# A macaron transformer block: order of the casts and seeds in the paired feed-forward phases, values first in the mixer, and the last head's casts placed a chunk later

## Chip, cores and metric

The kernel runs on one core of a Trainium2 chip. The metric is device time in microseconds (us) for one execution. Three runs of the kernel before took 935.04, 937.92 and 938.45 us, median 937.92 us.

## What is computed

One block for 512 tokens of width 1024, all float32: half a SwiGLU feed-forward network of width 2816, a token mixer with eight heads, again half a feed-forward network, and an RMS norm.

```python
def swiglu(x, w_gate, w_up, w_down):
    return (jax.nn.silu(x @ w_gate) * (x @ w_up)) @ w_down

x = x + 0.5 * swiglu(rmsnorm(x, ffn1_norm[layer]), ...)
x = x + token_mixer(rmsnorm(x, mix_norm[layer]), w_in[layer], w_out[layer], ...)
x = x + 0.5 * swiglu(rmsnorm(x, ffn2_norm[layer]), ...)
return rmsnorm(x, final_norm)
```

In the mixer `x @ w_in` gives queries, keys and values. Four differential heads form `a = p0 - lam * p1` from two softmaxes with a relative bias and apply it to the values (`oa`, followed by an RMS norm per head). Eight small heads sum three dilated attention branches (`ob`). The concatenated heads are multiplied with `w_out`.

## The kernel before

**Arithmetic.** Activations lie transposed, as eight tiles `x[0]` to `x[7]` of 128 features by 512 tokens. To keep float32 accuracy each operand is split in a high part (a cast to the reduced type, on ScalarE, `A`) and a low part (the operand minus that cast, on VectorE, `V`). A product is then three matmuls on TensorE (`T`): high by high, high by low, low by high (`mm3`, L124 to L126). So every weight needs a cast and a subtraction before its phase: `high` (L383) and `low` (L387) in the feed-forward networks, `high` (L854) and `low` (L858) in the mixer.

**Feed-forward networks (`ffn`).** After some ordinary units the network works on pairs of row blocks with seven half-width products in place of eight, a Winograd scheme. One unit has seven phases of 12 matmuls of 256 columns each:

```python
SEVEN = (("a11", "w", "b11"), ("s3", "z", "t3"), ("s2", "x", "t2"), ("a12", "w", "b21"),
         ("s1", "y", "t1"), ("a22", "x", "t4"), ("s4", "y", "b22"))
```

The first name is the weight block or sum, the second the PSUM bank (`pw`, `px`, `py`, `pz`) that it accumulates in, the third the activation block. After a11 bank w is copied as a seed into bank x, and after s2 bank x into bank y (`A.copy`, reported at L412). So s2 waits for the first seed and s1 for the second; s4, which accumulates in y, also waits until VectorE has read y after s1 (L415 in a gate or up unit, L424 in an output unit). Units come as `("g", j)` gate, `("u", j)` up, `("p", m)` plain output and `("d", group, m)` paired output. All of it is put in order by a list of planned times: `at(time, rank, f)` pushes a step on a heap, `put` is rank 0, `starts[t]` is the planned start of phase t, and `STEP` (1410 ns) the planned length of a phase. Steps come out by time, then by rank, then by the order in which they were pushed, and each engine runs its own steps in that order. Nothing waits for the planned time itself. At one time the ranks before are: 0 the reading of banks, seeds, activations and casts of gated results; 1 loads and the low parts `t0_rest` and `t1_rest`; 2 weight sums (`total`, L365 and L367) and the gate's `silu` of bank w; 2.5 `low`; 3 `high`; 4 `product`, the matmuls. `high` stands four steps ahead of its phase and `low` three.

In a gate unit `silu(0, left)` reads bank w a step after a12, and `silu(1)` the sum in `res["bc"]` a step after a22; the up unit multiplies them in later (`mul`, `stt`). `kept` makes the operands of the output units from the gated result. There `t0_parts` (reported at L557) casts a difference that VectorE has just formed (L421).

**Mixer.** The work is a list of chunks of 6 matmuls of 512 columns (queries and keys, `qk_chunks`, 8 chunks for each of `q0` to `q7`) or 12 of 256 columns (values, `v_chunks`, 8 for each of `v0` to `v3`), in the order of `plan`. Chunk c of `v_chunks` computes token block `c // 2` with weight half `c % 2`, so one bank is in work at a time. Around the chunks events are placed by chunk number: `put(t, rank, f)`, ranks below 10 ahead of the chunk, others behind it. After each chunk one half of a weight unit is cast (`high`) and the low part of the one before is formed.

After the chunks of `q{u}`, `scaled` brings queries and keys out of PSUM with the norm's factors (tq at L933, tk at L935, VectorE). Then heads 0 and 7 (`DIRECT`) run `evac_now`: four casts for each of two halves (L965, L967, L968 and L970) on ScalarE, and two subtractions for each (L966, L969) on VectorE, all queued right behind the last chunk. The other heads run `evac_q` (four casts) and `evac_k` (two subtractions of keys, L956, two of queries, L959, and copies between partitions by DMA). `attention(u, s)` then places scores (`sc`, L1002 and L1003), the biased row maximum with its subtraction (L1005, VectorE), the exponential (L1008, ScalarE), `combine` (L1012 to L1019), `turn` (transposes `pt`, L1026, and their copy `ptb`, L1029, ScalarE), `values` (`po`, L1039), `scale`, `finish` (`ot`, L1075, and the cast of `mh`) and `finish_low`. Head u starts at chunk s; its strips of the bias are loaded by two DMAs of SyncE's queue at chunk s - 3. Scores use two PSUM buffers, and so do transposes.

`means` and `spread` (`rstd`) work out the norm's factors. `means` makes the column `col` that scales the values and the diagonal `dg`; `spread` multiplies `dg` with ones (`bc_n`, L193) and copies the result to `bc`, which scales queries and keys. They stand at chunks 3 and 6.

After the last queries come `w_out` chunks (`pwo`) between which the last two heads run. The casts of some later `w_out` units (L115, L116) are placed by the scheduler of the framework, not by the list.

Of the kernel before, what the change touches and what calls it, by code (L numbers as in the profile page):

```python
# [65 lines left out]
def tile_macaron(ctx: ExitStack, tc, xs, xT, wf, wgu1, wst1, wd1, wdg1, wqk, wv, wo, wgu2, wst2, wd2,  # L66
# [132 lines left out]
    def ffn(wgu, wst, wd, wdg, n0, n1, norm, early, res, nm, hooks, ended, first=None,  # L199
# [206 lines left out]
        def put(time, f, *a):  # L406
            at(time, 0, f, *a)
# [18 lines left out]
        def product(t):  # L426
            u, o = ops[t]
            h, l = made.pop(t)
            if o[0] == "p":
                m = u[1]  # L430
                po = mm_bank(f"pd{nm}{m}")
                for k in range(PLAIN):
                    c = slice(k * P, (k + 1) * P)
                    mm3(po[:], h[:, c], l[:, c], ah[k][:], al[k][:], k == 0, k == PLAIN - 1)
                put(starts[t + 1], stt, x[m], po[:], 0.5, x[m], ALU.add)
                return
            if t == begin[u]:
                made[u] = {}
                for b, tag in zip("wxyz", bank_tags(u)):
                    made[u][b] = pp.tile([P, S], F32, tag=tag, name=f"p{b}{u[0]}{nm}{t}",  # L440
                                         bufs=4 if tag == "mm" else 2)[:, :HS]
            banks = made[u]
            seeded = o[0] not in ("a11", "s3")
            if t == 0 or ops[t - 1][1][0] == "p":
                T.matmul(banks[o[1]][:, :P], h[:, :P], moving(u, o[2])[0][0][:, :P],
                         start=True, stop=False, skip_group_check=True)
            for p, mv in enumerate(moving(u, o[2])):
                c = slice(p * P, (p + 1) * P)
                mm3(banks[o[1]], h[:, c], l[:, c], *mv, not seeded and p == 0, p == 3, seeded)


            if o[0] == "a11":
                put(starts[t + 1], A.copy, banks["x"], banks["w"])
            elif o[0] == "s2":
                put(starts[t + 1], A.copy, banks["y"], banks["x"])
            elif u[0] == "d":
                down_step(starts[t + 1], u, o[0], banks)
            else:
                pair_step(starts[t + 1], u, o[0], banks)
# [8 lines left out]
        def pair_step(t, u, o, banks):  # L468
# [15 lines left out]
            elif u[0] == "g":  # L484


                if o == "a12":
                    if j == n1:
                        put(t, silu, 0, left, pw)
                        put(t + STEP, times_up, 0, left)  # L490
                    else:
                        at(t + STEP, 2, silu, 0, left, pw)
                elif o == "s1":
                    put(t, add, res["bc"][:, right], py, p7)
                elif o == "a22":
                    put(t, add, p7, px, p7)
                    put(t + STEP * (j > n1), silu, 1, slice(0, S), res["bc"][:], -1.0)
                elif o == "s4":
                    put(t, silu, 0, right, py)
                    if j == n1:  # L500
# [16 lines left out]
        def kept(j, t1, t0, t2):  # L517
# [61 lines left out]
            put(n, less, g0[:, left], g0[:, left], g0[:, right])  # L579
            put(n + STEP, b2_rest)  # L580
            put(n + STEP, less, g0[:, right], g1[:, right], g0[:, right])
            put(n + 2 * STEP, t0_parts)
            put(n + 2 * STEP, stt, g1[:, right], g1[:, right], -1.0, g0[:, left], ALU.subtract)
            put(n + 2 * STEP, stt, g1[:, left], g1[:, right], -1.0, g1[:, left], ALU.subtract)

# [27 lines left out]
        def pipeline():  # L613
            seen = {}
            for t, (u, o) in enumerate(ops):
# [4 lines left out]
                else:  # L620
# [13 lines left out]
                    if o[0] in ("s2", "s4"):  # L634
                        at(starts[t] - 5 * STEP, 2, total, t)
                    at(starts[t] - 4 * STEP, 3, high, t)
                    at(starts[t] - 3 * STEP, 2.5, low, t)
                at(starts[t], 4, product, t)
            if bias is not None:
                at(starts[begin["p", 5]], 5, bias[0])  # L640
# [187 lines left out]
    V.tensor_scalar_mul(sub8[:], sm[:, 4 * KD:4 * KD + 1], 1.0 - LAM0)  # L828


    plan = ["q0", "v0", "q1", "v1", "q2", "q3", "q4", "v2", "q5", "q6", "v3", "q7"]
    v_end = [8 * plan.index(f"v{u // 2}") + 8 for u in range(8)]
    at = {}

# [43 lines left out]
    def v_chunks(qr):  # L878
# [2 lines left out]
        st = {}  # L881

        def chunk(c):
            i, kh = c // 2, c % 2
            if c == 0:
                ahead(us[0])
            if kh == 0:
                st["ps"] = mm_bank(f"pv{qr}{i}")
            po = st["ps"][:, :256]
            wh, wl = ready[us[kh]]  # L890
            xs = slice(i * P, (i + 1) * P)
            if c == 0:
# [6 lines left out]
            if kh == 1:  # L899
                if hf == 0:  # L900
                    vt[vi, i] = slot(vi * 4 + i, f"v{vi}{i}")
                A.activation(vt[vi, i][:, hf * 256:hf * 256 + 256], po, AF.Copy,
                             scale=held["col"][:, i:i + 1])
            if c == 7:
                ahead(us[1])
        return [lambda c=c: chunk(c) for c in range(2 * NQ)]

# [3 lines left out]
    def qk_chunks(u):  # L911
# [48 lines left out]

        def evac_now():
            q0, q1, k0, k1, l0, l1 = tiles()
            tq, tk = scaled()
            for a, b, qx, kx, lx in ((lo, hi, q0, k0, l0), (hi, lo, q1, k1, l1)):
                A.copy(qx[a, :], tq[a, :])  # L965
                V.tensor_tensor(qx[b, :], tq[a, :], qx[a, :].bitcast(F32), op=ALU.subtract)  # L966
                A.copy(kx[a, :], tk[a, :])  # L967
                A.copy(kx[b, :], tk[a, :])  # L968
                V.tensor_tensor(lx[a, :], tk[a, :], kx[a, :].bitcast(F32), op=ALU.subtract)  # L969
                A.copy(lx[b, :], lx[a, :].bitcast(F32))  # L970

        e = 8 * plan.index(f"q{u}") + 7
        if u in DIRECT:
            put(e, 11, evac_now)
        else:
            put(e, 11, evac_q)
            put(e + 1, 11, evac_k)
# [4 lines left out]
    def attention(u, s):  # L982
# [39 lines left out]
        def turn(m, i):  # L1022
# [3 lines left out]
                T.transpose(pt[:, k * P:(k + 1) * P],  # L1026
                            st["pr"][m][:, OFF[i] + k * P:OFF[i] + (k + 1) * P], ident[:])
            ptb = tp.tile([P, S], F32, tag="ptb", name=f"ptb{u}{m}{i}", bufs=2)
            A.copy(ptb[:, :w], pt[:, :w])  # L1029
            st["ptb", m, i] = ptb  # L1030

        def values(m, i):
# [63 lines left out]
        for i in range(NQ):  # L1096
# [2 lines left out]
            put(s + step * i + (1 if quick else 3), 5, combine, i)  # L1099
            if diff:  # L1100
                put(tv + 2 * i, 2, turn, 0, i)
                put(tv + 2 * i + 2, 1, values, 0, i)
            else:
                for m in range(2):
                    put(tv + step * i + (0 if quick else m), 2, turn, m, i)
# [11 lines left out]
        else:  # L1117
            put(e, 7, scale)
        put(e + (0 if quick else 2), 11 if quick else 3, finish)
        put(e + (0 if quick else 3), 12 if quick else 8, finish_low)  # L1120

    for w in plan:
        chunks += (qk_chunks if w[0] == "q" else v_chunks)(int(w[1]))
        if w[0] == "q":
            attention(int(w[1]), len(chunks) + (3 if int(w[1]) in DIRECT else 5))

    WO = 3
    wo_units = [unit(wo[m], f"wo{m}") for m in range(KD)]
# [19 lines left out]

    means, spread = rstd("n2", held)
    put(3, 9, means)  # L1150
    put(6, 9, spread)

    load(0)
    load(1)
# [215 lines left out]
```

## Time and profile before

| | |
|---|---|
| median of three runs | 937.92 us |
| the profiled execution, own time | 934.85 us |
| its span, first to last instruction | 933.1 us |
| VectorE busy | 723.9 us (78%) |
| ScalarE busy | 532.0 us (57%) |
| DMA moved | 136.71 MB, mean 147 GB/s |

In the rows of the trace the first number is the start in us from the beginning of the span and the second the duration. PE is TensorE, DVE is VectorE, ACT is ScalarE and SP is SyncE. A bracket at the end names idle time of that engine ahead of the row and what ended it. Matmuls overlap: a row's end is modelled, so the distance between two starts tells more than a duration. The stages by time: first feed-forward network to about 341 us, mixer to about 560, then the rest of `w_out` and the second network, whose paired phases run from 647 to 919 us, and the final norm.

### The profile page before, as it was taken

How to read it: one execution, taken by the hardware profiler on the slowest of the kernel's cores; microseconds unless marked ns; L12 is line 12 of the kernel's file. 1: busy time of each engine (PE TensorE's matmuls, PEld its weight loads, DVE VectorE, ACT ScalarE, POOL GpSimd, SP SyncE). 2: the span in 40 equal slices, each digit the busy share in tenths (PEclk: the TensorE clock that was granted, in tenths of full speed). 3: DMA queues.
4: the chain of work that ended last, by engine and by line, in shares of the span. 5: the costliest groups of instructions: out<-in, count | busy, mean ns of one | idle time of the engine just before them, and what ended most of it. 6: DMA issues, size and time to landing. Idle time of an engine off the chain costs nothing.

```text
span 933.1 us, 17213 instructions
## 1 busy us (share of the span) xinstructions
PE 916.4 (98%) x6462; PEld 848.4 (91%) x6462; DVE 723.9 (78%) x1490; ACT 532.0 (57%) x1102; POOL 98.3 (11%) x117
## 2 busy tenths in 40 slices
PE   9999999999999999999999999999999999999995
PEld 7788999999999998988989888888999899999995
DVE  6697897687997896668764537597899778798786
ACT  7455664355664665566756645355666445666462
POOL 0011101112102100000000002201110102220100
PEclk9999999999999999999999999999999999999997
DMA  7176646578757641443333103345775667874832
GB/s 251 65 194 157 167 127 176 137 195 223 195 150 193 188 128 65 131 136 113 91 113 92 68 23 117 121 136 142 177 171 137 175 168 178 216 215 124 209 103 91
DMA packets 60388, 136.71 MB, mean 147 GB/s; under 512 B 6848, under 2 KB 9152, under 8 KB 60304
## 3 DMA queue, kind: packets, MB, share of 16 engines
q1 hardware_dynamic: 46304, 110.14, 35.8%
q0 software_dynamic: 14000, 25.47, 17.4%
q8 instruction: 50, 0.82, 0.4%
q14 instruction: 34, 0.28, 0.1%
HBM read 130.30 MB, written 2.14 MB: 142 GB/s over the span
## 4 chain that ended last, share of the span: by engine, by line
PE 91%; DVE 6%; ACT 2%; issue 1%; DMA 1%; SPq 0%; DVEq 0%
PE po L1039 3%; PE pwo L124 1%; PE pwo L125 1%; PE pwo L126 1%; PE pua L126 1%; PE pua L125 1%; PE pua L124 1%; PE pv L896 1%; PE pv L897 1%; PE pv L898 1%; PE pt L1026 1%; PE pq L124 1%; PE pq L126 1%; PE pq L125 1%; PE pdb L124 1%; PE pda L124 1%
## 5 line engine op out<-in xcount | busy, mean ns | idle before, releaser
L1005 DVE CUSTOM_DVE_ANT_0 pr<-sc,strip 128x128 f32<-128x128 f32 (+3 forms) x64 | 30.9, 488 | 34.8 <-PE sc L1003 34.2
L1008 ACT ACTIVATE pr<-pr,small 128x128 f32<-128x128 f32 (+3 forms) x64 | 36.0, 563 | 32.1 <-DVE small L1005 31.2
L383 ACT CAST w<-s2b 128x512 fp32r<-128x512 f32 x50 | 31.1, 622 | 14.1 <-DVE s2b L365 12.7
L383 ACT CAST w<-s2a 128x512 fp32r<-128x512 f32 x46 | 28.7, 623 | 15.9 <-DVE s2a L365 13.3
L151 POOL TENSOR_TENSOR sq<-sq,sqt 128x512 f32<-128x512 f32 x7 | 10.9, 1559 | 254.4 <-ACT sqt L150 254.4
L387 DVE TENSOR_TENSOR w<-s2b,w 128x512 fp32r<-128x512 f32 x50 | 34.3, 686 | 4.3 <-ACT w L383 4.3
L1039 PEld LDWEIGHTS po<-v,ptb 128*128 128x128 f32 x240 | 32.7, 191 | 5.3 <-ACT ptb L1029 2.7
L896 PE MATMUL pv<-w,xh 128*128 128x256 f32 x128 | 35.9, 281 | 0.0
L897 PE MATMUL pv<-w,xl 128*128 128x256 f32 x128 | 35.8, 280 | 0.0
L898 PE MATMUL pv<-w,xh 128*128 128x256 f32 x128 | 35.7, 279 | 0.0
L387 DVE TENSOR_TENSOR w<-s2a,w 128x512 fp32r<-128x512 f32 x46 | 31.5, 686 | 3.9 <-ACT w L383 3.9
L1039 PE MATMUL po<-v,ptb 128*128 128x64 f32 (+1 forms) x240 | 32.5, 269 | 1.8 <-ACT ptb L1029 1.7
L1029 ACT COPY ptb<-pt 128x128 f32<-128x128 f32 (+3 forms) x48 | 20.0, 424 | 20.2 <-PE pt L1026 19.9
L124 PE MATMUL pq<-xh,w 128*128 128x512 f32 x64 | 26.9, 421 | 0.0
L124 PE MATMUL pwo<-mh,w 128*128 128x512 f32 x64 | 26.1, 407 | 0.0
L125 PE MATMUL pwo<-ml,w 128*128 128x512 f32 x64 | 25.5, 399 | 0.0
L126 PE MATMUL pwo<-mh,w 128*128 128x512 f32 x64 | 25.5, 398 | 0.0
L124 PE MATMUL pk<-xh,w 128*128 128x512 f32 x64 | 25.1, 393 | 0.0
L125 PE MATMUL pq<-xl,w 128*128 128x512 f32 x64 | 25.1, 392 | 0.0
L126 PE MATMUL pq<-xh,w 128*128 128x512 f32 x64 | 25.1, 392 | 0.0
L126 PE MATMUL pk<-xh,w 128*128 128x512 f32 x64 | 25.0, 391 | 0.0
L125 PE MATMUL pk<-xl,w 128*128 128x512 f32 x64 | 25.0, 390 | 0.0
(671 smaller groups left out, 3973.8 us busy)
## 6 DMA issues: line engine op xcount, KB each, us to landing
raw_qk<-wqk_dram SPq DMA_DIRECT2D x16, 512.0 KB, 3.5
raw0bg<-wst_dram SPq DMA_DIRECT2D x9, 512.0 KB, 4.6
raw_gua<-wgu_dram SPq DMA_DIRECT2D x8, 512.0 KB, 3.9
raw0ag<-wst_dram SPq DMA_DIRECT2D x8, 512.0 KB, 4.8
raw0ad<-wdg_dram SPq DMA_DIRECT2D x8, 512.0 KB, 5.0
strip<-bias_rows SPq DMA_DIRECT2D x16, 256.0 KB, 3.5
raw_v<-wv_dram SPq DMA_DIRECT2D x8, 512.0 KB, 3.2
raw_wo<-wo_dram SPq DMA_DIRECT2D x8, 512.0 KB, 3.2
```

The lines of the kernel that those rows point to most:

```text
L124: T.matmul(po, wh, mh, start=first, stop=False, skip_group_check=on)
L125: T.matmul(po, wh, ml, start=False, stop=False, skip_group_check=on)
L126: T.matmul(po, wl, mh, start=False, stop=last, skip_group_check=on)
L383: A.copy(made[t][0], source(t))
L387: V.tensor_tensor(l, source(t), h.bitcast(F32), op=ALU.subtract)
L896: T.matmul(po, xh[k][:, xs], wh[:, o:o + 256], start=k == 0, stop=False)
L897: T.matmul(po, xl[k][:, xs], wh[:, o:o + 256], start=False, stop=False)
L898: T.matmul(po, xh[k][:, xs], wl[:, o:o + 256], start=False, stop=k == KD - 1)
L1005: V.tensor_tensor_reduce(out=pi, in0=ps[:, :w], in1=st["b"][m][:, w - 1::-1], op0=ALU.add, op1=ALU.min, scale=1.0, scalar=3.0e38, accum_ou ...
L1008: A.activation(pi, pi, AF.Exp, scale=-1.0, bias=st["mx"][:, m, i:i + 1], accum_out=st["ls"][:, m, i:i + 1])
L1029: A.copy(ptb[:, :w], pt[:, :w])
L1039: T.matmul(st["po3"][:, i, d0:d0 + dn], st["ptb", m, i][:, k * P:(k + 1) * P], vt[u // 4, k][:, fo + d0:fo + d0 + dn], start=k == 0, stop= ...
```

## The change

Six edits. (1) In the paired phases the two seeds get rank -1, ahead of all else at their time; the gate's `silu(0, left)` goes from rank 2 to 3.5, behind the weight casts; `silu(1)` goes one step later in all units but the first; `t0_parts` goes behind the other rank 0 steps. (2) The `low` of an a11 phase, unless the phase before is a plain unit, goes from three steps ahead at rank 2.5 to two steps ahead at rank 0.5. (3) The mixer starts with `v0`: its chunks run over the four token blocks with the first weight half, then over the four with the second, in four banks; its second unit's preparation is called after chunk 3. `spread` goes from chunk 6 to chunk 10. Head 0 starts at chunk 20 in place of 11. (4) The last `values` of head 1 goes a chunk later. (5) `evac_now` makes the two last casts (L970) behind all others; for head 7 `scaled` stays behind the last chunk, and the rest of `evac_now` goes a chunk on, behind that chunk's `turn`. (6) The last `ptb` copy of head 6 goes to VectorE, and head 6's `finish_low` a chunk earlier.

```diff
             if o[0] == "a11":
-                put(starts[t + 1], A.copy, banks["x"], banks["w"])
+                at(starts[t + 1], -1, A.copy, banks["x"], banks["w"])
             elif o[0] == "s2":
-                put(starts[t + 1], A.copy, banks["y"], banks["x"])
+                at(starts[t + 1], -1, A.copy, banks["y"], banks["x"])
...
-                        at(t + STEP, 2, silu, 0, left, pw)
+                        at(t + STEP, 3.5, silu, 0, left, pw)
...
-                    put(t + STEP * (j > n1), silu, 1, slice(0, S), res["bc"][:], -1.0)
+                    put(t + 2 * STEP * (j > n1), silu, 1, slice(0, S), res["bc"][:], -1.0)
...
-            put(n + 2 * STEP, t0_parts)
+            at(n + 2 * STEP, 0.5, t0_parts)
...
-                    at(starts[t] - 3 * STEP, 2.5, low, t)
+                    if o[0] == "a11" and t and ops[t - 1][1][0] != "p":
+                        at(starts[t] - 2 * STEP, 0.5, low, t)
+                    else:
+                        at(starts[t] - 3 * STEP, 2.5, low, t)
...
-    plan = ["q0", "v0", "q1", "v1", "q2", "q3", "q4", "v2", "q5", "q6", "v3", "q7"]
+    plan = ["v0", "q0", "q1", "v1", "q2", "q3", "q4", "v2", "q5", "q6", "v3", "q7"]
...
-            i, kh = c // 2, c % 2
+            i, kh = (c % 4, c // 4) if qr == 0 else (c // 2, c % 2)
...
-                st["ps"] = mm_bank(f"pv{qr}{i}")
-            po = st["ps"][:, :256]
+                st[i] = mm_bank(f"pv{qr}{i}")
+            po = st[i][:, :256]
...
-            if c == 7:
+            if c == (3 if qr == 0 else 7):
                 ahead(us[1])
...
-            tq, tk = scaled()
+            tq, tk = scaled() if u != 7 else (st["tq"], st["tk"])
             for a, b, qx, kx, lx in ((lo, hi, q0, k0, l0), (hi, lo, q1, k1, l1)):
...
                 V.tensor_tensor(lx[a, :], tk[a, :], kx[a, :].bitcast(F32), op=ALU.subtract)
+            for a, b, lx in ((lo, hi, l0), (hi, lo, l1)):
                 A.copy(lx[b, :], lx[a, :].bitcast(F32))
...
-        if u in DIRECT:
+        if u == 7:
+            put(e, 11, scaled)
+            put(e + 1, 2.5, evac_now)
+        elif u in DIRECT:
             put(e, 11, evac_now)
...
-            A.copy(ptb[:, :w], pt[:, :w])
+            if (u, m, i) == (6, 1, NQ - 1):
+                V.tensor_copy(ptb[:, :w], pt[:, :w])
+            else:
+                A.copy(ptb[:, :w], pt[:, :w])
...
-                put(tv + 2 * i + 2, 1, values, 0, i)
+                put(tv + 2 * i + (3 if (u, i) == (1, NQ - 1) else 2), 1, values, 0, i)
...
-        put(e + (0 if quick else 3), 12 if quick else 8, finish_low)
+        if u == 6:
+            put(e + 2, 9, finish_low)
+        else:
+            put(e + (0 if quick else 3), 12 if quick else 8, finish_low)
...
-            attention(int(w[1]), len(chunks) + (3 if int(w[1]) in DIRECT else 5))
+            attention(int(w[1]), len(chunks) + (3 if w == "q7" else 4 if w == "q0" else 5))
...
     put(3, 9, means)
-    put(6, 9, spread)
+    put(10, 9, spread)
```

## The prediction

> **What bounds the kernel now.** I read the page first: span, then the chain that ended last.
>
> ```profile
> span 933.1 us, 17213 instructions
> PE 91%; DVE 6%; ACT 2%; issue 1%; DMA 1%; SPq 0%; DVEq 0%
> ```
>
> TensorE carries 91% of the chain, so only time in which it stands still can be won. The diff takes no matmul away. Next I read busy time by stages.
>
> ```profile
> 305.00:342.00 37.00, 36.62 (x307) 35.42 (x307) 35.38 (x71) 25.83 (x50) 2.91 (x4) 1.00 0.55 161
> 650.00:913.00 263.00, 263.00 (x2178) 257.34 (x2177) 221.01 (x408) 156.25 (x318) 36.87 (x43) 1.00 0.66 168
> ```
>
> After the length of the stage, the columns are PE, its weight load, DVE, ACT, POOL, the granted clock and DMA. The second network's paired phases have no gap at all: 263.00 us for 2178 matmuls, 0.12 us each. So what can be won lies in the first network's paired phases and in the mixer. I went through the timeline of PE there, looking for distances between starts that are longer than the normal ones. The longest gap is in the last head.
>
> ```profile
> 531.81 1.00 PE L1039 MATMUL po<-v,ptb 128*128 128x64 f32 x8
> 532.62 0.47 PE L124 MATMUL pwo<-mh,w 128*128 128x512 f32 x1
> ...
> 533.63 0.39 PE L125 MATMUL pwo<-ml,w 128*128 128x512 f32 x1
> 533.86 0.40 PE L126 MATMUL pwo<-mh,w 128*128 128x512 f32 x1
> 535.94 1.10 PE L1039 MATMUL po<-v,ptb 128*128 128x64 f32 x8 [1.69 <-ACT ptb L1029]
> ...
> 540.14 0.60 PE L124 MATMUL pwo<-mh,w 128*128 128x512 f32 x1
> ...
> 544.90 0.33 PE L1026 MATMUL pt<-ident,pr 128*128 128x128 f32 x1 [0.59 <-ACT ptb L1029]
> ```
>
> Values of head 6 wait for a turned block. Its copy stands in ScalarE's queue behind the whole evacuation of head 7:
>
> ```profile
> 529.60 0.62 ACT L965 CAST q<-tq 64x512 fp32r<-64x512 f32 x1 [0.78 <-DVE tq L933]
> ...
> 535.32 0.57 ACT L1029 COPY ptb<-pt 128x512 f32<-128x512 f32 x1
> ```
>
> After that wait TensorE runs at about half its clock for a while (the 0.53 is the granted clock):
>
> ```profile
> 537.40:540.80 3.40, 3.40 (x11) 2.82 (x11) 1.72 (x7) 0.51 (x3) 0.00 (x0) 0.53 0.37 123
> ```
>
> **The change part by part.** The last head first (edits 5 and 6). From 533.86 to 540.14 passed 6.28 us. The same work without a stop: the matmul at 533.86, 0.23 (distance from 533.63); eight `po`, 0.81 (531.81 to 532.62); six `pwo`, 1.47 (532.62 to 533.86 and 0.23 more); four `sc` of 256 columns at 0.12, 0.48. That is 2.99, so **3.29** are lost: a wait of 535.94 - 533.86 - 0.23 = 1.85 and 1.44 of half rate. In the new order VectorE makes that copy, behind tq and tk. Its nearest row is VectorE's copy of the same shape out of PSUM:
>
> ```profile
> 352.30 0.69 DVE L195 COPY rbc_n<-bc_n 128x512 f32<-128x512 f32 x1 [0.62 <-PE bc_n L193]
> ```
>
> So it ends near 531.3, long before 534.1, when the values want it. The copy delays VectorE's four subtractions by 0.69. ScalarE's eight casts start at 529.60 as before, since they wait for tq and not for the chunk; at 0.62 and a little between them eight take some 5.1, and a scheduler-placed weight cast of 0.62 can come between: 534.7 to 535.4. The scores want them at 534.09 + 0.81 + 1.47 = 536.4. What hides the later casts is thus one `w_out` chunk; a miss costs its own length and perhaps the half rate again (first rival). The 0.59 at 544.90 goes too if `finish_low` of head 6, now ahead of the next two turns, has freed a transpose buffer: I take **0.59**, between 0 and 0.59.
>
> Edits 3 and 4, the mixer's start:
>
> ```profile
> 351.14 1.12 PE L193 MATMUL bc_n<-dg_n,ones_m 128*128 128x512 f32 x2 [0.34 <-DVE dg_n L189]
> ```
>
> ```profile
> 362.13 0.69 DVE L858 TENSOR_TENSOR w<-raw_qk,w 128x512 fp32r<-128x512 f32 x1 [0.19 <-ACT w L854]
> ```
>
> ```profile
> 363.08 0.39 PE L1002 MATMUL sc<-k,q 128*128 128x256 f32 x1 [0.45 <-DVE small L1005]
> ```
>
> ```profile
> 414.18 0.39 PE L126 MATMUL pk<-xh,w 128*128 128x512 f32 x1
> 414.70 1.16 PE L1039 MATMUL po<-v,ptb 128*128 128x128 f32 x8
> ```
>
> A bracket counts from the modelled end; a 512-column row shows 0.39 and starts every 0.23, a 256-column one 0.28 and 0.12, so 0.16 is added to each bracket. `bc_n` waits 0.34 + 0.16 = **0.50** for the diagonal; four chunks later it is long there. The score at 363.08 waits 0.61 for a row maximum that stands behind the subtraction at 362.13, which waits for ScalarE, busy with head 0's casts. Its matmul also takes 0.11 more than one in full run (0.39 for 0.28): **0.72**. Head 0 gets four chunks of 6 x 0.23 = 1.4 us in place of three, 1.4 for a wait of 0.6. The values at 414.70 start 0.52 after a matmul that needs 0.23, and get a whole chunk more: **0.29**. Costed at nothing, because matmul work of the same amount covers it: the values' new order (the second weight half comes four chunks in, as with q0), the four banks (their last readers are a whole unit back), and the strips of head 0. These two DMAs on SyncE's queue move with the head and still go out three chunks, 4.1 us, ahead:
>
> ```profile
> strip<-bias_rows SPq DMA_DIRECT2D x16, 256.0 KB, 3.5
> ```
>
> Uncovered, a late strip would cost up to that 3.5 once.
>
> Something is late next: head 0 now meets q1's evacuation, as head 2 meets q3's:
>
> ```profile
> 428.64 1.41 DVE L959 TENSOR_TENSOR q<-tq,q 64x512 fp32r<-64x512 f32 x2
> 430.08 0.56 DVE L1005 CUSTOM_DVE_ANT_0 pr<-sc,strip 128x384 f32<-128x384 f32 x1
> ```
>
> ```profile
> 430.70 0.50 PE L1002 MATMUL sc<-k,q 128*128 128x512 f32 x1 [0.23 <-DVE small L1005]
> ```
>
> There a score waits 0.23 + 0.16 = 0.39 because the row maximum stands behind the subtractions of `evac_k`, and ScalarE's exponentials and the blocks to be turned wait behind that. I add **0.4** for head 0, between 0 and three such waits, 1.2, taking one since one is what head 2 shows.
>
> Edits 1 and 2, the paired phases:
>
> ```profile
> 99.97 0.28 PE L126 MATMUL pwga<-xh,w 128*128 128x256 f32 x1
> 100.36 0.39 PE L124 MATMUL pyga<-txa,w 128*128 128x256 f32 x1
> ...
> 103.71 0.39 PE L124 MATMUL pyga<-xh,w 128*128 128x256 f32 x1 [0.33 <-DVE rbc_n L415]
> ```
>
> ```profile
> 99.42 0.62 ACT L557 CAST h3a<-g0a 128x512 fp32r<-128x512 f32 x1 [0.90 <-DVE g0a L421]
> ```
>
> ```profile
> 102.63 0.69 DVE L387 TENSOR_TENSOR w<-raw0au,w 128x512 fp32r<-128x512 f32 x1
> ```
>
> ```profile
> 330.06 0.39 PE L124 MATMUL pyda<-h1a,w 128*128 128x256 f32 x1 [0.38 <-DVE x L424]
> ```
>
> ```profile
> 328.99 0.68 DVE L387 TENSOR_TENSOR w<-raw0ad,w 128x512 fp32r<-128x512 f32 x1
> ```
>
> At 100.36 the seed for bank y came late because a `t0_parts` cast, itself waiting 0.90 for VectorE, stood ahead of it. With rank -1 it is ahead: 0.39 - 0.12 + 0.11 = **0.38**. At 103.71 and 330.06 s4 waits until bank y is read, and the read stands right behind the `low` of the next a11 (102.63 and 328.99), 0.6 to 0.7 long. That `low` now comes behind it. The waits, 0.33 + 0.16 + 0.11 = **0.60** and 0.38 + 0.16 + 0.11 = **0.65**, are no longer than what is taken away. The other shifts of edit 1 I cost at nothing: the results of both `silu` are multiplied several phases later, and the weight casts run four steps ahead. If that cover fails, a phase waits for a cast of 0.6.
>
> Sum: 3.29 + 0.59 + 0.50 + 0.72 + 0.29 + 0.38 + 0.60 + 0.65 = 7.02, less 0.4, is 6.62. Against the execution's own 934.85 that gives 928.23. The median of the runs is 937.92, 3.07 above it, so I add half of that, 1.5: **929.7**.
>
> **The rivals.** First, the last head's stall only moves: the scores of head 7 wait for the last low copies. For it speaks that 534.7 to 535.4 leaves 1.0 to 1.7 on paper, and that scheduler-placed casts may shift; against it, that the casts still start with tq. With a wait of 1.0 and 1.44 of half rate, 2.4 come back: 930.7, with the 1.5 932.2.
>
> Second, heads 0 and 1 crowd ScalarE and VectorE in chunks 24 to 31 (casts of q1, exponentials, turned copies, values out of PSUM), and a turned block is late as at 535.94. One such wait of 1.85 and two of 0.39 are 2.6 against the 0.4 taken, 2.2 more: 930.4, with 1.5 931.9. For it speaks that the waits of heads 1 and 2 show both queues as the releaser; against it, that PE has 1.4 us for each chunk.
>
> Third, the half rate isn't caused by the wait and stays, shifted: 1.44 come back, 929.7, with 1.5 931.2. The row speaks against it: 0.53 right behind the only long wait. [...]
>
> Fourth, on the other side: the `low` of a11, moved to two steps ahead, comes too late for its matmuls. It is done in 42 phases (20 in the first network, 22 in the second), most of them in stages without a gap.
>
> ```profile
> 682.35 0.68 DVE L387 TENSOR_TENSOR w<-raw0bu,w 128x512 fp32r<-128x512 f32 x1
> 682.95 0.41 DVE L415 TENSOR_TENSOR rbc_n<-pygb,rbc_n 128x256 f32<-128x256 f32 x1
> ```
>
> ```profile
> 684.88 0.28 PE L124 MATMUL pwub<-xh,w 128*128 128x256 f32 x1
> ```
>
> It now ends at 683.03, 1.85 ahead of its phase. Exchanged with the read of 0.41 it ends 0.4 later, with 1.4 to spare. It decides only once VectorE runs more than 1.4 behind, for which the 35.38 busy us of 37.00 at the end of the first network speak. At a price of 0.3 for each, 42 x 0.3 = 12.6 against 6.62: 940.8, with 1.5 942.3. From 0.16 each on the kernel is slower than before.
>
> Fifth, the change does nothing that can be measured: waits fall but others of the same length come, 937.9. Eight independent gaps speak against it.
>
> **How the numbers follow.** Forecast 0.60, last head moved 0.13, heads crowded 0.10, half rate stays 0.07, a11 late 0.06, nothing 0.04. The range reaches from 926.5 (934.85 less all 7.02 is 927.8, and 1.3 for switches of PE that I did not count) to 935.0 (the first two rivals together, 928.2 + 2.4 + 2.2 + 1.5 = 934.3, rounded up). Something over 0.5%, 4.7 us, can be told from no change here, so faster means under 933.2. The forecast holds it nearly always (0.57), the first three rivals mostly (0.16 of 0.30): faster 0.73; the fourth and a little more: slower 0.07; the rest, 0.20, the same.
>
> **What would show it.** In the profile of the changed kernel: no wait of `po` for `ptb` near 534, a granted clock near 1.00 through the last head, `ptb` once from VectorE, and scores of head 7 without an idle bracket; no bracket at `bc_n`; at most one new bracket at `sc` of head 0; the three gaps of the first network's paired phases gone, and the second network's as dense as before. A bracket at the first matmul after the moved casts in the last head, or brackets at L126 of a11 phases, would make the prediction wrong.

## The result, and the profile after

In the same group of runs the changed kernel took 929.09 us (median of 6 runs, 926.16 to 930.04) and the kernel before 938.18 us (6 runs, 935.04 to 941.67): ratio 0.9904, 95% interval 0.988 to 0.9929. The forecast was 929.7 us. The profiled execution took 930.04 us, for 934.85 before. First the page of the changed kernel: the span, and the shares of the chain that ended last.

```profile
span 928.3 us, 17216 instructions
PE 92%; DVE 5%; issue 1%; ACT 1%; DMA 1%; SPq 0%; DVEq 0%; ACTq 0%
```

TensorE bounds it as before. The last head, by the timelines of PE, DVE and ACT of the changed kernel (three fences):

```profile
533.52 0.39 PE L126 MATMUL pwo<-mh,w 128*128 128x512 f32 x1
533.75 1.00 PE L1049 MATMUL po<-v,ptb 128*128 128x64 f32 x8
...
536.03 0.28 PE L1009 MATMUL sc<-k,q 128*128 128x256 f32 x1
...
536.50 0.40 PE L124 MATMUL pwo<-mh,w 128*128 128x512 f32 x1
...
540.18 0.48 PE L1033 MATMUL pt<-ident,pr 128*128 128x128 f32 x2
```

```profile
530.36 0.69 DVE L1037 COPY ptb<-pt 128x512 f32<-128x512 f32 x1 [0.44 <-PE pt L1033]
```

```profile
529.26 0.62 ACT L968 CAST q<-tq 64x512 fp32r<-64x512 f32 x1 [0.78 <-DVE tq L936]
...
533.72 0.62 ACT L115 CAST w<-raw_wo 128x512 fp32r<-128x512 f32 x1
534.36 0.62 ACT L974 CAST l<-l 64x512 fp32r<-64x512 f32 x1
```

The values at 533.75 wait for nothing. From 533.52 to 536.50 pass 2.98 us where 6.28 passed before, so 3.30 are won (3.29 forecast). The copy ends at 531.05, the last low cast at 534.98 (forecast 534.7 to 535.4, with a weight cast between, as there is). The transposes at 540.18 follow each other without the wait of 0.59: from the start of the one to that of the other pass 0.18, for 0.86 before. The clock in this stretch, by busy time and granted clock (third number from the end):

```profile
533.80:537.20 3.40, 3.40 (x22) 3.00 (x21) 2.37 (x6) 2.29 (x4) 0.00 (x0) 1.00 0.00 0
```

What TensorE still waits for in the changed kernel (total, times, longest):

```profile
PE sc L1009 <- DVE small L1012: 0.4, 1, 0.4
PE pyda L124 <- DVE x L424: 0.3, 1, 0.3
PE pyga L124 <- DVE rbc_n L415: 0.2, 1, 0.2
```

The waits of `bc_n` at the mixer's start, of head 0's score and of head 1's values are gone, and the new wait of 0.4 for head 0 didn't come: the one `sc` is that of head 2, as before. The `pyga` is the s4 at 103 us, which was to lose its wait. VectorE, then TensorE:

```profile
101.71 0.68 DVE L527 TENSOR_TENSOR h4a<-g0a,h3a 128x512 fp32r<-128x512 f32 x1
102.31 0.68 DVE L365 TENSOR_TENSOR s2a<-s1au,raw0au 128x512 f32<-128x512 f32 x1
102.91 0.42 DVE L415 TENSOR_TENSOR rbc_n<-pyga,rbc_n 128x256 f32<-128x256 f32 x1
```

```profile
103.39 0.39 PE L124 MATMUL pyga<-xh,w 128*128 128x256 f32 x1 [0.19 <-DVE rbc_n L415]
103.61 0.28 PE L125 MATMUL pyga<-xl,w 128*128 128x256 f32 x1
103.73 0.28 PE L126 MATMUL pyga<-xh,w 128*128 128x256 f32 x1
```

The `low` is no longer ahead of the read, but a weight sum and a subtraction of the first output operands are. The whole ledger, by the starts of the same matmul in both traces (the first or the last of its name):

| up to the start of | before | after | gained in this part | forecast | gained in a later run, `again` below |
|---|---|---|---|---|---|
| first `pwda` | 173.93 | 175.79 | -1.86 | 0.98 | 1.49 |
| last `pyda` | 341.37 | 342.70 | 0.53 | 0.65 | 0.55 |
| first `pwo` | 530.35 | 530.01 | 1.67 | 1.11 | 1.67 |
| last `sc` | 548.68 | 544.14 | 4.20 | 3.88 | 4.20 |
| last `pydb` | 919.42 | 914.86 | 0.02 | 0 | 0.06 |
| end | 933.08 | 928.27 | 0.25 | 0 | 0.22 |

The mixer and the last head gained 0.56 and 0.32 more than forecast. The 0.53 of the second part comes near its 0.65 by luck: the wait of 0.65 us at 330 us went, one of 0.60 at 341 us came, and the rest is a short stretch of slow matmuls that the execution before had from 334.4 to 341.3. The first part lost 1.86. There the waits fell, as shown; the matmuls themselves were slower. Two windows of 10 us without a wait, before and then after:

```profile
105.00:115.00 10.00, 10.00 (x91) 10.00 (x90) 7.95 (x15) 6.33 (x14) 1.73 (x2) 1.00 0.79 193
```

```profile
105.00:115.00 10.00, 10.00 (x85) 10.00 (x84) 7.92 (x16) 6.06 (x13) 1.76 (x2) 1.00 0.83 201
```

The 10 us hold 91 matmuls of 256 columns in the one and 85 in the other (those cut by an end of the window are counted), both at a granted clock of 1.00. The rows from 103.61 on have the slow pace: 0.12 us from start to start in place of 0.1133 (12 in 1.44 us, not 1.36). A distance of 117 to 124 ns between two such matmuls of the paired phases is called a slow step below, and a long run of them a stretch. In the profiled execution of the changed kernel one stretch begins at 103.6 and ends at 155.1, where a plain unit with 512 columns begins. In all that execution has 481 slow steps, 3.17 us more than at 113.3 ns each. In that of the kernel before it was 228 steps, 1.44 us. The difference, 1.73, is about what the profile lacks of the forecast 6.6: it gained 4.8.

### The profile page after: what moved, and what is told of

It is laid out like the page before. It is cut to its first block, busy times and chain, and to the rows that moved or that the text cites. A ratio compares the mean times of both kernels' runs of the same rounds, so it can differ in the third digit from the quotient of the medians.

```text
span 928.3 us, 17216 instructions
## 1 busy us (share of the span) xinstructions
PE 915.8 (99%) x6462; PEld 849.7 (92%) x6462; DVE 722.6 (78%) x1491; ACT 532.7 (57%) x1101; POOL 98.4 (11%) x117
## 4 chain that ended last, share of the span: by engine, by line
PE 92%; DVE 5%; issue 1%; ACT 1%; DMA 1%; SPq 0%; DVEq 0%; ACTq 0%
PE po L1049 2%; PE pv L899 2%; PE pv L900 2%; PE pv L901 2%; PE pwo L124 2%; PE pwo L125 2%; PE pwo L126 2%; PE pua L125 1%; PE pua L124 1%; PE pua L126 1%; PE pt L1033 1%; PE pda L126 1%; PE pda L124 1%; PE pub L126 1%; PE pdb L124 1%; PE pda L125 1%
## 5 line engine op out<-in xcount | busy, mean ns | idle before, releaser
L861 DVE TENSOR_TENSOR w<-raw_qk,w 128x512 fp32r<-128x512 f32 x32 | 21.7, 687 | 5.3 <-ACT w L857 5.3
```

The costliest lines, as they stand in the source:

```text
L861: V.tensor_tensor(l[:, c:c + 512], raw[:, c:c + 512], h[:, c:c + 512].bitcast(F32), op=ALU.subtract)
```

## The experiments

Each kernel was run in five rounds (one in three) against the kernel before. The kernels of one group ran on one chip, the four groups on different ones. The last column of each table gives the slow steps of the profiled execution and what they took over 113.3 ns each.

### First group: one part of the change each

Before: 936.70 us (931.89 to 942.49). `p_last` has edits 5 and 6 alone, `p_mixer` edits 3 and 4, `p_paired` edits 1 and 2, `again` is the changed kernel.

> The kernel before with edits 5 and 6 alone. Theory (the gap in the last head is ScalarE's queue, and the half rate follows the wait): no wait of po for ptb, granted clock near 1.00 through the last head, 3.29 + 0.59 = 3.9 us less, ratio near 0.996. Rival (the half rate is not caused by the wait): the wait goes, matmuls at half rate remain, 1.85 + 0.59 = 2.4 us less, ratio near 0.9975. Rival (the stall only moves to the scores): 1.5 us less.

> The kernel before with edits 3 and 4 alone. Theory: the brackets at bc_n, at the first sc and at the last po of head 1 go, 0.50 + 0.72 + 0.29 = 1.5 us less, less 0 to 0.4 for a new wait of head 0: ratio 0.9984 to 0.9988. Rival (heads 0 and 1 crowd each other): new brackets at sc or po between chunks 24 and 31, no gain or up to 1 us more.

> The kernel before with edits 1 and 2 alone. Theory: the waits near 100, 103 and 330 us go or shrink, 1.0 to 1.6 us less. In the profile of the changed kernel 35 phases from 103 to 154 us took 1.44 us in place of 1.36, against 12 in the kernel before; if that belongs to the order of the paired phases, it is here too and takes 1.8 us back, so that no gain is left (ratio 1.000); if it comes and goes with the run, it need not be here, and the ratio is 0.9985.

> The changed kernel, unaltered, a second time. If the slow phases (1.44 us for 1.36) belong to the order, they fill 103 to 154 us here as well; if they come and go with the run, their number is another one, and the profiled time differs from the first by 0.08 us for each phase. Ratio as before, 0.988 to 0.993.

| | median us (range) | ratio to before, 95% | slow steps, us over 113.3 ns each |
|---|---|---|---|
| `p_last` | 930.62 (928.84 to 936.06) | 0.9953 (0.993 to 0.9977) | 998, 6.6 |
| `p_mixer` | 935.93 (930.77 to 943.17) | 0.9998 (0.9968 to 1.0028) | 1798, 12.0 |
| `p_paired` | 930.85 (930.24 to 934.31) | 0.9942 (0.9917 to 0.9966) | 57, 0.3 |
| `again` | 926.53 (926.16 to 926.97) | 0.9903 (0.9874 to 0.9931) | 54, 0.3 |

The last head alone gives 4.4 us (interval 2.2 to 6.6); its profile shows neither the wait nor a lower clock:

```profile
532.00:537.00 5.00, 5.00 (x30) 4.29 (x29) 3.90 (x11) 3.19 (x6) 0.00 (x0) 1.00 0.00 0
```

The mixer's gain of some 1.5 us can't be read from its time: its profiled execution, which has lost all three waits, holds four slow stretches, and its runs spread over 12 us. In its trace the mixer's part of the ledger is 1.67 us shorter. The paired phases gave 5.4 us (3.2 to 7.8) where their waits are worth 1.6; neither ratio that was expected (1.000 or 0.9985) came. So the slow pace was the thing to explain. In `p_mixer` one stretch begins here (TensorE, then VectorE):

```profile
686.17 0.28 PE L126 MATMUL pxgb<-ttb,w 128*128 128x256 f32 x1
686.29 0.28 PE L124 MATMUL pygb<-xh,w 128*128 128x256 f32 x1
686.41 0.28 PE L125 MATMUL pygb<-xl,w 128*128 128x256 f32 x1
```

```profile
685.12 0.69 DVE L387 TENSOR_TENSOR w<-raw0bu,w 128x512 fp32r<-128x512 f32 x1
685.72 0.41 DVE L415 TENSOR_TENSOR rbc_n<-pygb,rbc_n 128x256 f32<-128x256 f32 x1
```

It is an s4 phase of a gate unit. Nothing is seen to wait, but VectorE's read of bank y, behind the `low` of a11, ended at 686.13, only 0.16 ahead of the matmul that needs it. This time from the end of the read to the start of s4 is called the margin below. The long stretches in the second network, in `p_last` and `p_mixer`, all begin at such phases (677.9, 686.3, 815.6, 824.0). In the order of the changed kernel the read is first. VectorE in `again`, where s4 starts at 675.58, 0.59 after the read's end:

```profile
674.57 0.42 DVE L415 TENSOR_TENSOR rbc_n<-pygb,rbc_n 128x256 f32<-128x256 f32 x1
674.90 0.69 DVE L387 TENSOR_TENSOR w<-raw0bu,w 128x512 fp32r<-128x512 f32 x1
```

### Second group: the paired phases in two parts, the last head in two parts

Before: 934.60 us (932.26 to 936.12). `p_low` is the kernel before with edit 2 alone, `p_ranks` with edit 1 alone. `x_copy_act` and `x_evac_early` are the changed kernel with these edits:

```diff
-            if (u, m, i) == (6, 1, NQ - 1):
-                V.tensor_copy(ptb[:, :w], pt[:, :w])
-            else:
-                A.copy(ptb[:, :w], pt[:, :w])
+            A.copy(ptb[:, :w], pt[:, :w])
```

```diff
-            put(e + 1, 2.5, evac_now)
+            put(e, 11, evac_now)
```

> The kernel before with edit 2 alone (the low of a11 two steps ahead, behind the read of bank y). Theory: TensorE takes 12 half-width matmuls in 1.44 us instead of 1.36 for about 430 matmuls at a time, and such a stretch starts at an s4 phase of a gate unit for which VectorE's read of bank y after s1 ended only just in time (0.05 to 0.16 us ahead). Edit 2 alone puts the read ahead of the subtraction of 0.69, so the margin at those s4 phases grows from 0.16 to about 0.58, and no stretch starts in the second network; at most the s4 near 103 us, whose margin is small for another reason, can still start one. Ratio 0.994 to 0.996, most of what edits 1 and 2 together gave (0.9942), and a narrow spread of the runs (under 5 us). Rival: the ranks of edit 1 (seeds ahead, silu later) stop the slow stretches, and edit 2 takes away only the two waits of 0.60 and 0.65: ratio 0.9987, spread as wide as before (about 10 us), slow stretches in the profile.

> The kernel before with edit 1 alone (seeds at rank -1, both silu later, t0_parts later). Theory: the subtraction still stands ahead of the read of bank y, so the margin at the s4 phases of gate units stays near 0.16, slow stretches of about 430 matmuls at 1.44 us per 12 still come in some executions, and only the wait of 0.38 at 100 us goes: ratio 0.999 to 1.000, runs spread over some 8 to 11 us. Rival: the ranks stop the slow stretches: ratio 0.994 to 0.996, narrow spread, no step of 1.44 us in the profile.

> The changed kernel with the seventh pair's last turned block copied by ScalarE again, so the rest of edit 5 and 6 alone (tq and tk first, casts a chunk later, low copies last). Theory: the copy needs no VectorE, since it is the casts' place a chunk later that frees it: it stands ahead of the casts and ends near 530.5, values don't wait and the granted clock stays 1.00; the casts start about 1.7 us later (near 530.9 instead of 529.3), the last low cast ends near 536.5 instead of 535.0, and the second half's scores wait 0 to 0.6. Ratio to the changed kernel 1.000 to 1.0007, that is 926.5 to 930 us. Rival (the prediction's): the copy on VectorE is what takes the wait away, and without it the values wait again with half rate behind: 3.3 us back, 930 to 933 us.

> The changed kernel with the rest of head 7's evacuation put back right behind the last chunk, the copy of the turned block left on VectorE. Theory: VectorE's copy now stands behind the four subtractions, which wait for the casts; it ends near 533.5 to 534.5 instead of 531.05, and the values wait 0 to 1.0; ScalarE's casts end as before. Ratio to the changed kernel 1.000 to 1.001. If the wait reaches 1.69 again, the half rate behind it should come back too: 2 to 3 us. Rival: it is the copy's engine alone that decides, and its place in the queue doesn't matter: no wait, same time.

| | median us (range) | ratio to before, 95% | slow steps, us over 113.3 ns each |
|---|---|---|---|
| `p_low` | 932.99 (931.33 to 935.51) | 0.9983 (0.9971 to 0.9996) | 102, 0.6 |
| `p_ranks` | 933.49 (932.55 to 934.62) | 0.9993 (0.9983 to 1.0003) | 267, 1.7 |
| `x_copy_act` | 927.29 (926.76 to 929.49) | 0.9927 (0.9911 to 0.9944) | 61, 0.4 |
| `x_evac_early` | 926.96 (926.54 to 929.44) | 0.9925 (0.9906 to 0.9943) | 64, 0.4 |

The margin did what was expected (`p_low` 0.58 at the gate units' s4, `p_ranks` 0.15), but on this chip the kernel before spread over 4 us only, so there seems to have been little pace to win: `p_low` missed its 0.994 to 0.996 and came near its rival's 0.9987, and of the 11 s4 phases of `p_ranks` with a margin of 0.15 none began a long stretch. This pair decides nothing about the pace. It tells something of the waits. `p_low` has none at 103 us, `p_ranks` a longer one there, 0.90 over the normal distance for 0.50 before: edit 1, not edit 2, keeps a wait at that place.

In the last head each half of the change does nearly all alone: by the traces the part of the last head is 0.7 us longer than in `again` in `x_copy_act` and 0.4 in `x_evac_early`, of the 4.2 won. With the copy on ScalarE, ahead of the casts that now come a chunk later, the values don't wait. A score does, 0.30 over the normal distance, and a transpose, 0.48 (0.12 in the changed kernel), for a bank that VectorE reads late (ScalarE, then TensorE of `x_copy_act`):

```profile
526.92 0.59 ACT L1036 COPY ptb<-pt 128x512 f32<-128x512 f32 x1 [1.86 <-PE pt L1033]
527.40 0.62 ACT L968 CAST q<-tq 64x512 fp32r<-64x512 f32 x1
```

```profile
537.67 0.30 PE L1033 MATMUL pt<-ident,pr 128*128 128x128 f32 x1 [0.27 <-DVE ml L1097]
```

With the evacuation at its old place and the copy on VectorE, behind the four subtractions (VectorE, then TensorE of `x_evac_early`), the values wait 0.33 over the normal distance:

```profile
529.45 0.69 DVE L1037 COPY ptb<-pt 128x512 f32<-128x512 f32 x1
```

```profile
530.20 1.10 PE L1049 MATMUL po<-v,ptb 128*128 128x64 f32 x8 [0.16 <-DVE ptb L1037]
```

What costs is both together, the copy on ScalarE and the evacuation ahead of it, as in the kernel before, where the values waited 1.85 us. The rival of `x_copy_act`, the prediction's reading that VectorE's copy takes the wait away, falls: it is enough, not needed. `p_low` also shows that the clock doesn't fall behind each such wait. It still has the old last head, with the stop of 1.87 us:

```profile
532.00:537.00 5.00, 3.29 (x20) 2.56 (x19) 3.49 (x7) 3.46 (x6) 0.00 (x0) 1.00 0.00 0
540.00:545.00 5.00, 4.41 (x26) 3.62 (x26) 3.00 (x10) 3.40 (x12) 0.00 (x0) 1.00 0.00 0
```

`p_mixer` has the same stop, and behind it this:

```profile
540.00:545.00 5.00, 5.00 (x21) 4.14 (x20) 2.05 (x9) 0.92 (x4) 0.00 (x0) 0.66 0.29 105
```

Of five profiled executions with the stop two show half rate behind it (a granted clock of 0.53 over 3.4 us before, 0.66 over these 5 us in `p_mixer`) and three don't (1.00 in each 5 us from 530 to 545 in `p_paired`, `p_low` and `p_ranks`). Without the stop none does: 1.00 in each 5 us from 525 to 550 in all nine profiles of the new last head.

### Third group: the margin by itself, the fourth rival, the waits left

Before: 934.30 us (932.24 to 940.10). All three are the changed kernel with one or two edits: in `x_edge` the gate units' read of bank y stands behind the `low` of the next a11 again,

```diff
                 elif o == "s1":
-                    put(t, add, res["bc"][:, right], py, p7)
+                    at(t, 0.7, add, res["bc"][:, right], py, p7)
```

in `x_a11_later` that `low` is one step ahead of its phase,

```diff
-                        at(starts[t] - 2 * STEP, 0.5, low, t)
+                        at(starts[t] - STEP, 0.5, low, t)
```

and in `x_both` the first pair's operands come a step later, and `evac_k`'s two subtractions of queries have an event of their own:

```diff
-            late = 2 * STEP * (j > n1)
+            late = STEP * (2 if j > n1 else 1)
...
+            put(e + 2, 11, evac_k_q)
```

> The changed kernel with two more edits: (a) t0_rest and t1_rest of the first pair a step later, so that the casts and subtractions of the first output operands no longer stand ahead of the reading of bank y at 102 us; (b) the two query subtractions of evac_k behind the chunk, apart from the two key subtractions, so that a row maximum of the next head does not queue behind them. Theory: the gap of 0.35 us at 102 us and the one of 0.57 at 426 (score waiting for a row maximum) are gone, nothing takes their place: 0.6 to 0.9 us less than the changed kernel, ratio to it 0.9990 to 0.9994; the margin at the s4 near 103 us grows from 0.05 to 0.3 or more, so no slow stretch can start there. Rival for (a): the subtractions that move a step later are then late for their own product or collide with the next reading, and the gap comes back within 2 us of the place: same time. Rival for (b): the queries are late for their scores: a wait of 0.5 or more of sc for q, same time or slower.

> The changed kernel with edit 2 undone for the gate units alone: their reading of bank y after s1 stands behind the low of the next a11 again. Theory: the margin at s4 of gate units falls from 0.58 to 0 to 0.16 us, and on a chip where the kernel before spreads by 8 us or more, slow stretches (12 half-width matmuls in 1.44 us) come back at these phases in most executions: median 1 to 5 us above the changed kernel (926.5 to 927 where it was run again), spread of 3 to 9 us; on a chip where the kernel before spreads by only 4 us, stretches are rare and only real waits count, 0 to 2 us. Rival: the slow stretches have nothing to do with this margin, but with the mixer or with the seeds: time and spread as the changed kernel, under 2.5 us.

> The changed kernel with the low of a11 only one step ahead of its phase, in place of two: the prediction's fourth rival brought about. Theory: the low then ends some 0.5 us after the phase has begun and its third matmul waits 0.3 to 0.7 us in each of the 42 phases (the weight's low part is wanted by the third matmul): 12 to 29 us more than the changed kernel, 939 to 956 us, brackets of that size at L126 of a11 phases. Rival: TensorE is behind VectorE by enough, or the framework starts the phase's other matmuls first, so that nothing is lost: 926 to 929 us.

| | median us (range) | ratio to before, 95% | slow steps, us over 113.3 ns each |
|---|---|---|---|
| `x_both` | 927.43 (927.10 to 927.49) | 0.9927 (0.9915 to 0.9939) | 46, 0.3 |
| `x_edge` | 934.53 (929.85 to 938.48) | 1.0004 (0.9987 to 1.002) | 1110, 7.4 |
| `x_a11_later` | 935.40 (933.97 to 936.44) | 1.0012 (1.0002 to 1.0023) | 464, 2.7 |

`x_edge` decides: with the order of two VectorE operations in the gate units put back, the slow steps return and the whole gain is lost. Its rival, that the stretches come from the mixer or the seeds, falls. Beside `again` its profiled execution is 8.7 us longer: 7.1 are slow steps (7.4 for 0.3), 0.4 a longer wait at 103 us, and 1.3 come at seven other s4 phases, which start 0.07 late and whose second matmul comes 0.11 late. The median is 7.1 us above that of `x_both`, which differs little from the changed kernel, where 1 to 5 were expected. One start (VectorE, then TensorE, then two windows, ahead of it and behind it):

```profile
679.05 0.69 DVE L387 TENSOR_TENSOR w<-raw0bu,w 128x512 fp32r<-128x512 f32 x1
679.65 0.42 DVE L415 TENSOR_TENSOR rbc_n<-pygb,rbc_n 128x256 f32<-128x256 f32 x1
```

```profile
679.94 0.28 PE L126 MATMUL pxgb<-ttb,w 128*128 128x256 f32 x1
680.12 0.39 PE L124 MATMUL pygb<-xh,w 128*128 128x256 f32 x1
680.35 0.28 PE L125 MATMUL pygb<-xl,w 128*128 128x256 f32 x1
680.47 0.28 PE L126 MATMUL pygb<-xh,w 128*128 128x256 f32 x1
```

```profile
670.00:680.00 10.00, 10.00 (x91) 10.00 (x89) 9.90 (x21) 6.86 (x14) 0.03 (x1) 1.00 0.61 140
682.00:692.00 10.00, 10.00 (x86) 10.00 (x85) 7.92 (x15) 6.14 (x14) 2.42 (x3) 1.00 0.76 188
```

The read ends at 680.07, s4 starts at 680.12, 0.07 later than it would; from there on the pace is 0.12, to 731.8. The margin here, 0.05, is tighter than the 0.16 of the kernel before. Not each such start does it: of 8 s4 phases of gate units with 0.05 or 0.06 in this execution four began a stretch. Counted over all 14 profiles, leaving out phases inside a stretch already running, this many began one of 90 slow steps or more:

| margin at the s4 of a gate unit, us | phases | began a stretch |
|---|---|---|
| 0.05 or 0.06 | 20 | 7 |
| 0.10 to 0.17 | 42 | 5 |
| 0.28 and more | 155 | 0 |

That the order of the two operations brings the stretches is shown by `x_edge`. That it does so by the margin is argued from this count (11 of the 42 are of the fourth group's `x_reset`, whose short matmuls may also hinder a start). Four more stretches began elsewhere: one in `p_ranks` behind a wait in an output unit, three in `x_a11_later`.

`x_a11_later` shows where the fourth rival begins to decide. One step later than in the change it costs 8 us beside `x_both`; the list of waits of TensorE has it:

```profile
PE pwga L126 <- DVE w L387: 2.2, 5, 1.2
...
PE pwgb L126 <- DVE w L387: 1.5, 6, 0.3
PE pwua L126 <- DVE w L387: 0.2, 1, 0.2
```

It is 12 phases, not 42: 11 at the start of gate units, mostly 0.42 over the normal distance and once 1.32, and one up unit, 5.9 us together. In the others VectorE is early enough even so. Three slow stretches begin right behind such waits. The expectation of 12 us and more was too high by the phases that don't wait.

`x_both` loses the wait at 102 (0.35 over the normal distance) and that of 0.54 at head 2's score, but the next score waits 0.28. A new wait of 1.26 comes at 422.42, of a matmul for keys, for VectorE's read of a head's result. The read ends at 422.27, for 421.33 in `again`: the subtractions of head 1's queries, moved, stand at 412.58 behind an operation for which VectorE waits 1.84, and all that follows on VectorE up to this read is later by some 0.9:

```profile
PE pk L124 <- DVE ob L1079: 1.1, 1, 1.1
```

So (a) held, (b) cost more than it won, as its rival said though at another operation, and the 0.6 to 0.9 us that were expected didn't come.

### Fourth group: what ends the slow pace

Before: 937.41 us (932.34 to 940.20). `x_reset` is `x_edge` with a matmul of 128 columns ahead of each paired unit:

```diff
-            if t == 0 or ops[t - 1][1][0] == "p":
+            if t == begin[u]:
                 T.matmul(banks[o[1]][:, :P], h[:, :P], moving(u, o[2])[0][0][:, :P],
```

> The kernel of x_edge (reading of bank y behind the low of a11 in gate units) with one matmul of 128 columns ahead of the first matmul of every paired unit; it stood ahead of a unit only where the one before was plain, so 42 are added. What it writes is overwritten by the matmul behind it. Theory: a slow stretch is a state of TensorE's stream of equal 256-column matmuls, and a matmul of another shape ends it. The next a11 comes one phase after s4, so a stretch lasts 12 to 13 matmuls at most and costs 0.1 us: at most 150 slow steps (1110 in x_edge), spread under 3 us, and the time is that of the changed kernel, 926.5 to 927, and 0.4 for the wait at 102 us, and 42 matmuls of 0.06 to 0.1 us, 2.5 to 4.2: 929.4 to 931.6. Rival: only the plain units' long matmuls (512 columns) or their stream end the state, not a short one between: stretches of 11 to 52 us as in x_edge, spread of 8 us, median 937 or more (934.5 and 2.5).

932.52 us (932.23 to 933.92, 12 runs), ratio 0.9959 (0.9944 to 0.9974); 139 slow steps, 0.7 us, no stretch. An s4 of the unit shown for `x_edge`, with the inserted matmul behind it, and the window behind that:

```profile
679.47 0.28 PE L124 MATMUL pygb<-xh,w 128*128 128x256 f32 x1
679.59 0.28 PE L125 MATMUL pygb<-xl,w 128*128 128x256 f32 x1
...
679.93 0.28 PE L125 MATMUL pygb<-xl,w 128*128 128x256 f32 x1
680.04 0.28 PE L126 MATMUL pygb<-xh,w 128*128 128x256 f32 x1
680.16 0.22 PE L445 MATMUL pwub<-xh,w 128*128 128x128 f32 x1
680.22 0.33 PE L124 MATMUL pwub<-xh,w 128*128 128x256 f32 x1
680.39 0.28 PE L125 MATMUL pwub<-xl,w 128*128 128x256 f32 x1
```

```profile
682.00:692.00 10.00, 10.00 (x91) 10.00 (x90) 8.22 (x16) 6.62 (x15) 1.72 (x2) 1.00 0.88 201
```

The spread is 1.7 us for 8.6 in `x_edge`, with the old order of VectorE. So with it long stretches didn't come in these runs. Whether the short matmul ends them or hinders their start stays open: it also moved the margin from 0.05 to 0.11, and at this s4 the pace was back to 0.11 before the short matmul came. It is no bargain: each costs 0.12 us (from 680.16 to 680.39 pass 0.23, where one matmul takes 0.11), 42 are 5.0, more than the 2.5 to 4.2 expected, and the time is above the 929.4 to 931.6 expected too.

## Why the prediction was right, and where not

- **Last head.** The wait, its size and its half rate were read rightly (3.29 forecast, 3.30 found). The transposes gave 0.68 in place of 0.59, and the matmul at 540.14, just outside the sum, was still slow by 0.19. The cause was told too narrowly: the move of the evacuation would have done without the copy on VectorE. And 1.44 of the 3.29, the half rate, belongs to some executions only (two of the five profiled with the stop).
- **Mixer.** 1.11 forecast, 1.67 found. The new wait of 0.4 taken over from head 2 didn't come.
- **Paired phases, waits.** The 0.38 at 100 us went. The 0.60 at 103 shrank by 0.14 only: the step "the read stands right behind the `low`" left out what else would stand there; `x_both` takes that away and the wait with it. The 0.65 at 330 went, and 0.60 came back at the last output unit, at 341 us (0.50, and 0.10 at the next matmul), the `pyda` in the list of waits. So next to nothing was won by this term.
- **Paired phases, pace.** The step that failed is "the second network's paired phases have no gap at all", from which followed that nothing could be won there and that the fourth rival alone could change it. For the execution that was read this is right: the 0.12 us each is a mean of 2032 matmuls of 256 columns at 0.113 and 144 of 512 at 0.227, and the part from the last `sc` to the last `pydb` took 370.74 us there, 370.69 in `again`. But one profile doesn't stand for all: in `p_last`, with the same paired phases as before, this part took 376.53 us, also without a gap. So matmuls came 6% slower there (0.12 for 0.1133) in a stage without a gap. This term was nil in the forecast. In the first group edits 1 and 2 gave 5.4 us for 1.63 forecast; in the second, where the kernel before spread less, the variants with most of the change stood at 0.9925 to 0.9927, some 6.9 us, near the 6.62 of the sum.
- **Rivals.** The last head's stall didn't move, heads 0 and 1 don't crowd, and the half rate is gone with its wait in every profile of the new last head (granted clock 1.00 in all nine). The `low` of a11 isn't late: in `again` it ends 1.31 to 1.50 ahead of its phase in 40 of the 42 phases and 0.95 ahead in the other two, for 1.4 forecast.
- **The sum.** 928.23 against the profiled execution stands between 930.04 (one slow stretch) and 926.66 (`again`, none). That 929.7 hit 929.09 is in part luck: the 1.5 us were added because the runs before spread, with no cause named. The slow pace of the kernel before was in the forecast by that, without a name.

## What to carry to other kernels

A wait that has shrunk to nothing was not yet safe here: of 62 s4 phases of gate units whose bank came free only 0.05 to 0.17 us ahead, 12 began a slow stretch, and a stretch of some 430 steps cost about 3 us, more than most of the waits. Where runs of one kernel spread by several us (10.6 here before, 0.8 in `again`), take more than one profile, compare the distance between equal matmuls in a stretch without gaps, and put the reads that free a bank ahead of work that has time (the other order put `x_edge` 7.1 us above `x_both`). To judge one part of a change, undo it inside the changed kernel too: `p_low` and `p_ranks`, built on the kernel before, told nothing of the pace on their chip, and `x_edge`, built on the changed one, told it plainly on another.

## What the hardware showed that was not expected

The pace: 256-column matmuls in one stream took 120 ns in place of 113.3, at a granted clock of 1.00, in 12 of 16 stretches of 90 steps or more from an s4 phase of a gate unit with a margin of 0.05 to 0.17 us, in the longest case some 430 steps in 52 us, up to the next plain unit. None of the 155 s4 of gate units with a margin of 0.28 or more began one. What in the engine holds this state no record shows. It differs by chip or by run: the kernel before spread over 10.6 us in one group and 3.9 in another.

The half rate: in two of five profiles a stop of about 1.85 us was followed by a granted clock of 0.53 over 3.4 us (the kernel before) and of 0.66 over 5 us (`p_mixer`); in the other three the clock stayed at 1.00. What decides between them no run shows.
